# Next block's x loaded into idle output places, and a reordered opening, in a fused matmul–GELU–matmul kernel

## The chip, the cores and the metric

The kernel runs on one core of one Trainium2 chip. Its metric is the device time in microseconds (us), median of several runs: 881.87 us before the change, from three runs between 881.13 and 882.86. A lower time is better.

The engines are named as the profile names them: PE is the matrix engine (PEld its weight loads), DVE the vector engine, ACT the scalar engine, POOL the GpSimd engine, SP the sync engine, which here only issues transfers. "SPq", "ACTq" and "POOLq" are the transfers that those three engines issue; each has one queue of transfers, and an engine issues them in its own program order. All queues use the same 16 DMA engines.

## The reference

```python
x: (16, 512, 768)   w1: (768, 3072)   b1: (3072,)   w2: (3072, 768)      # float32
y = np.matmul(x, w1) + b1
y = 0.5 * y * (1.0 + erf(y / np.sqrt(2.0)))          # exact GELU
return np.matmul(y, w2).astype(np.float32)
```

So 8192 rows of x go through a product, a bias, a GELU and a second product.

## The kernel before

**Blocks of rows.** The 8192 rows are cut into ten blocks of 768 rows (six tiles of 128) and a last one of 512. A block's x lies in SBUF transposed, as `xt` (bf16; there is one such buffer). The GELU's output lies in `g`, and the output of the second product is collected in `ot`, which has four places of 128 x 768 float32 each.

**First product.** Blocks 1 to 10 use a two-by-two Strassen-like scheme: seven products P1 to P7 (line 154) for each of 12 pairs of column groups j, on sums of parts of w1 and sums of parts of x. The sums of x (`sum_x`, into `xft`) are made by DVE, the sums of w1 once (`make_w1`), stored to DRAM (`w1f`) and streamed back through a ring of five slots (`fill_slot`, on the SP queue, once for each j). Block 0 and a part of block 1 use plain products (line 396) instead, while the sums of w1 are being formed. ACT applies bias and GELU (line 143).

**Second product.** Three row tiles make a group: G0 and G1 in each block. A group's three-by-three-by-two product takes 15 products M0 to M14 of eight matmuls each (line 229), which add up in a few PSUM banks. Seven of them open a bank (M14, M8, M4, M7, M6, M13, M5). After a product, `finish2` copies the bank into a half of an output place (ACT, line 102) or adds it there (DVE, line 109); after M3, M11 and M0 a whole row tile is stored by POOL (line 237). A bank is used again by a later product of the same group: M12 goes on in M4's bank, M2 in M14's, M1 in M13's, so M12 must wait until M4 has been copied out, and so on.

**Places.** Group G0 of every block keeps its row 1 in place 0, row 2 in place 3, row 3 in place 2; G1 keeps row 1 in place 2, row 2 in place 1, row 3 in place 0. The first writes into them are the copies: M4 writes the first half of row 3, M13 its second half, M14 the first half of row 2, M6 its second half.

**The next block's x.** `prepare_x` loads each of the next block's six tiles with POOL into `xb` (a pool of two buffers, float32 turned into bf16 on the way) and transposes it with a DMA transpose on the SP queue from `xb` into `xt`. I call the six transposes T0 to T5. They may only start when the last product that reads `xt` has run. A third load waits until T0 has freed its buffer, and so on. `prepare_x` is called after M14 of group G0 in blocks 1 to 9, and ahead of group G0's products in block 0. In block 0 the order of the opening products is different: M4, M14, M13, M8, M7, M6 are fed together, and their copies follow in that order.

**The opening.** x tiles 0 and 1 come as float32 into places 2 and 3 (one on the SP queue, one on the ACT queue), are cast by DVE, and are transposed by PE (`turn_x0`). Until they arrive PE runs filler matmuls on zeros (`busy(n)`). Tiles 2 to 5 and the weights come on the POOL queue. Block 0's first products (`first`, line 459) use the first half of the first weight group, and then go on as the pieces arrive.

**Stores of the w1 sums.** The first four sums are kept in idle memory and stored at the end of block 0's first product by four transfers that ACT issues (`waiting`).

The order of the work is written out by hand: each engine executes its instructions in the order of the program, and waits are put in by the framework wherever regions of memory overlap.

Of the kernel before, what the change touches and what calls it, by code (L numbers as in the profile page):

```python
# [9 lines left out]
BF16 = mybir.dt.bfloat16  # L10
# [23 lines left out]
def kernel(  # L34
# [40 lines left out]
    def inorder(ins):  # L75
        return tc.keep_in_program_order(ins)

    def dma(queue, out, in_):
        inorder(queue.dma_start(out=out, in_=in_))  # L79
# [199 lines left out]
        ns = w // P  # L279
        return n // ns, (n % ns) * P  # L280

    def prepare_x(r0, w):
        for n in range(2 * w // P):
            xb = xbp.tile([P, K], BF16, name="xb")
            dma(nc.gpsimd, out=xb[:], in_=xf[r0 + n * P:r0 + (n + 1) * P, :])
            half, c0 = place(w, n)
            inorder(nc.sync.dma_start_transpose(out=xt[:, :, half, c0:c0 + P], in_=xb[:]))

    def sum_x(k, w):
        a11, a12 = xt[:, :KH, 0, :w], xt[:, KH:, 0, :w]  # L290
# [57 lines left out]
    def make_w1():  # L348
        nonlocal made
        n = made  # L350
        made += 1
        j = order1[n]
        a = raw(j)
        area, o = stage[n]
        s = area[:, o:o + SLOT].rearrange("p (f kc c) -> p f kc c", f=7, kc=KH)
        copy("act", s[:, 0:2], a[:, 1:3])

        def one():
            add(s[:, 2], a[:, 1], a[:, 2])
            add(s[:, 3:5], a[:, 0:4:2], a[:, 1:4:2])  # L360

        def two():
            sub(s[:, 5], a[:, 2], a[:, 0])
            sub(s[:, 6], a[:, 1], a[:, 3])
            if n < 4:
                waiting.append(lambda: dma(nc.scalar, out=w1f[j], in_=area[:, o:o + SLOT]))
            else:
                dma(nc.sync if n < 6 else nc.gpsimd, out=w1f[j], in_=area[:, o:o + SLOT])
            formed.add(j)
            if j in (9, 10):  # L370
                where[seq.index(j)] = area[:, o:o + SLOT]

        return one, two
# [52 lines left out]
    ident32 = words(stf, 2432, P)  # L426
    xw = ot[:, 2:4, :]
    dma(nc.sync, out=xw[:, 0, :], in_=xf[0:P, :])
    dma(nc.sync, out=b1s, in_=b1.rearrange("(hc p) -> hc p", p=P))
    dma(nc.scalar, out=xw[:, 1, :], in_=xf[P:2 * P, :])  # L430
    load_w1(0, 0, KH)
    inorder(nc.vector.memset(warm, 0.0))
    inorder(nc.scalar.activation(out=b1t[:, 0:1], in_=warm[:, 0:1], func=ACTF.Gelu))
    busy(7)
    make_identity(nc, ident32)
    copy("pool", ident, ident32)
    load_x0(2)
# [41 lines left out]
    MIDDLE = ("M12", "M2b", "M10a", "M11a", "M11b")  # L479

    copy("dve", xb0[:, 0, :], xw[:, 0, :])
    copy("dve", xb0[:, 1, :], xw[:, 1, :])
    turn_x0(0, "dve")
    tb = bank()
    inorder(nc.tensor.transpose(out=tb[:, :HC], in_=b1s, identity=ident32[:HC, :HC]))
    copy("act", b1t[:], tb[:, :HC])
    turn_x0(1, "dve")
    busy(4)
    first(0, 0, KH)
    first(1, 0, KH)  # L490
    turn_x0(2, "dve")
# [38 lines left out]
    make_w2(7)  # L530
    for m in ("M1", "M3b", "M10a", "M10b", "M11a", "M11b"):
        gsum(blk[0], m)
    for f in waiting:
        f()


    ts = [[dict() for _ in range(HP)] for _ in pairs]
# [22 lines left out]
    for p, (r0, w) in enumerate(pairs):  # L560
        nxt = pairs[p + 1] if p + 1 < len(pairs) else None
        G0, G1 = blk
        blk = groups(p + 1) if nxt is not None else None
        full = len(G1["tiles"]) == 3

        if p > 0:
            js = seq[:HP - PLAIN] if p == 1 else list(range(HP))
            last = len(js) - 1
            more = []
            if p == 1:  # L570
                hcs = [hc for j in range(PLAIN) for hc in (j, HP + j)]
                for n, hc in enumerate(hcs):
                    if n in (0, 1, 3):
                        form_w1()
                    if n in (1, 2):
                        sum_x(2 * n - 2, w)
                        sum_x(2 * n - 1, w)
                    plain(hc, 0)
                    if n == len(hcs) - 1:
                        ahead(p)  # L580
                    plain(hc, 1)
                free_slots(PLAIN)
                more = [0, 1, 3]

            both = (G0, G1) if full else (G0,)
            todo = [(js.index(QH - 1) if QH - 1 in js else 0, f) for G in both for f in gsums(G, *EARLY)]
            todo += [(js.index(2 * QH - 1), f) for G in both for f in gsums(G, *MIDDLE)]
            if p == 1:
                todo[2:4] = [(3, f) for _, f in todo[2:4]]

            halves = []

            def fill(s):
                if s in more and not halves:
                    more.remove(s)
                    halves.extend(make_w1())
                    halves.append(None)
                if halves and halves[0] is None:
                    halves.clear()
                elif halves:  # L600
                    halves.pop(0)()
                    if len(halves) == 1:
                        halves.clear()
                        free_slots(PLAIN)
                    return
                if s <= last and todo and s > todo[0][0] + (p > 1 or todo[0][0] > 0):
                    todo.pop(0)[1]()

            def step1(s, m):
                if 0 <= s <= last:  # L610
                    product1(ts[p][js[s]], m, p, js[s], w)

            for s in range(last + 1):
                if s == 0:
                    order = ((0, "P2"), (0, "P4"), (-1, "P1"), (0, "P6"))
                elif s == 1:
                    order = ((0, "P7"), (1, "P5"), (0, "P2"), (1, "P3"), (0, "P4"), (0, "P6"))
                else:
                    order = ((0, "P1"), (0, "P7"), (1, "P5"), (0, "P2"), (1, "P3"), (0, "P4"), (0, "P6"))
                for d, m in order:  # L620
                    step1(s - d, m)
                    if m in ("P2", "P6"):
                        fill(s)
            step1(last, "P5")
            part2(G0, "M14", range(0, 5))
            step1(last, "P3")
            part2(G0, "M14", range(5, QC))
            finish2(G0, "M14")
            if nxt is not None:
                prepare_x(*nxt)  # L630
            rest(G0, "M8")
            rest(G0, "M4")
            run([f for _, f in todo] + gsums(G0, *LATE))
            rest(G0, "M7")
            qs = [h * QH + q for q in range(QH) for h in range(2)]
            part2(G0, "M6", qs)
            finish2(G0, "M6")
            part2(G0, "M13", qs)
            finish2(G0, "M13")
        else:  # L640
            raws = ("M4", "M14", "M13", "M8", "M7", "M6")
            prepare_x(*nxt)
            for c in range(QC - 1):
                for m in raws:
                    part2(G0, m, (c,))
            for m in raws:
                part2(G0, m, (QC - 1,))
                finish2(G0, m)

        due = (gsums(G1, *EARLY, *MIDDLE) if p == 0 else []) + (gsums(G1, *LATE) if full else [])  # L650

        def take(n):
            r = due[:n]
            del due[:n]
            return r

        middle(G0, lambda n: take(1) if n >= 5 else [])
        rest(G0, "M0")

        if full:  # L660
            run(take(9))
            for m in ("M14", "M8", "M4"):
                rest(G1, m)
            if p > 0:
                for k in range(4):
                    sum_x(k, nxt[1])
            for m in ("M7", "M6", "M13"):
                rest(G1, m)
            if p == 0:
                form_w1()  # L670
            middle(G1, lambda n: [form_w1] if p == 0 and n == 5 else [])
            if p > 0:
                ahead(p + 1)
            rest(G1, "M0")
        else:
            a = lambda k: block(G1, 0, k)
            d12, d13 = st[:, 4, :, :], st[:, 5, :, :]
            sub(d12, a(0), a(1))
            sub(d13, a(0), a(2))
            t = ot[:, G1["o"][2], :]  # L680
            for n, terms in enumerate(((("b31", a(2)), ("M4", a(1)), ("b11", d12)),
                                       (("M13", a(2)), ("b22", a(1)), ("b12", d13)))):
                ps = bank()
                for f, lhs in terms:
                    for c in range(QC):
                        inorder(nc.tensor.matmul(  # L686
                            out=ps[:, :NB], lhsT=lhs[:, c, :], rhs=w2t[:, c, WF[f], :],
                            start=(f == terms[0][0] and c == 0), stop=(f == terms[2][0] and c == QC - 1)))
                copy("act", t[:, n * NB:(n + 1) * NB], ps[:, :NB])
                store(t, G1["rows"][0], True, n * NB, (n + 1) * NB)  # L690
# [30 lines left out]
```

## Time and profile before

| what | value |
|---|---|
| median of three runs | 881.87 us |
| the profiled execution's own time | 880.96 us |
| its span | 879.2 us |
| PE busy | 870.6 us (99%) |
| DVE / ACT / POOL busy | 587.6 / 397.9 / 84.6 us |
| PE's clock | 0.999 of full speed |
| DMA, mean | 168 GB/s |

The span is the time from the first to the last instruction in the profile; the device time stands 1.8 us above it in the profiled execution. The profiled execution itself is 0.91 us below the median of the runs. PE busy at 99% with the full clock says that the kernel can only be made shorter by taking away matmuls, or by taking away the remaining moments in which PE waits. A change that adds a wait to PE makes it longer by as much.

### The profile page before, as it was taken

Reading aid. Unit: us, or ns where it says so; the run is one execution under the profiler, and the core shown is the slowest. Engines: PE = TensorE matmul, PEld = TensorE weight load, DVE = VectorE, ACT = ScalarE, POOL = GpSimd, SP = SyncE. Lnnn points to the kernel's source line nnn. Section 1 sums busy time; section 2 is a strip of 40 time slices with the busy share of each in tenths; the row PEclk is TensorE's granted clock in tenths of the full one; section 3 lists DMA queues with packets and bytes.
Section 4 is the critical chain, followed back from the end, with each engine's and each line's share of the span. In section 5 each row is a group of like instructions: output and inputs, shape, how many; then the busy total and the mean of one; then the engine's idle time right before and its main releaser. Section 6 shows DMA issues by size and latency. Waiting matters only on the chain.

```text
span 879.2 us, 14061 instructions
## 1 busy us (share of the span) xinstructions
PE 870.6 (99%) x5505; PEld 532.6 (61%) x5505; DVE 587.6 (67%) x1105; ACT 397.9 (45%) x788; POOL 84.6 (10%) x153
## 2 busy tenths in 40 slices
PE   8999999999999999999999999999999999999998
PEld 6665556666666666666666666666666666666774
DVE  2888777757765766677577666756765766577654
ACT  3741384157227613741671276147316712751560
POOL 6201110110100011000001100110100011000000
PEclk9999999999999999999999999999999999999999
DMA  9998588566836664664668276556646683662621
GB/s 198 207 230 157 211 294 237 102 194 194 157 103 207 207 126 131 201 175 101 192 211 171 70 217 196 118 146 209 155 103 211 197 167 90 206 190 72 204 72 72
DMA packets 89031, 147.31 MB, mean 168 GB/s; under 512 B 50796, under 2 KB 68228, under 8 KB 88964
## 3 DMA queue, kind: packets, MB, share of 16 engines
q1 hardware_dynamic: 64148, 93.91, 37.2%
q0 software_dynamic: 24096, 49.36, 24.8%
q10 hardware_dynamic: 720, 3.15, 1.1%
q8 instruction: 43, 0.70, 0.3%
q14 instruction: 24, 0.20, 0.1%
HBM read 123.19 MB, written 33.42 MB: 178 GB/s over the span
## 4 chain that ended last, share of the span: by engine, by line
PE 93%; DMA 2%; DVE 2%; ACT 1%; issue 1%; POOL 0%; DVEq 0%; POOLq 0%; ACTq 0%
PE ps L229 44%; PE ps L154 42%; PE ps L396 5%; PE ps L686 1%; ACT g L143 1%; DMA w1f<-st 1%; PE ps L459 1%; DMA out_dram<-ot 1%; DMA ot<-in_x_dram 0%; DVE ot L109 0%; DMA xt<-xb 0%; ACT ot L102 0%; DVE st L112 0%; PE ps L421 0%; DVE ps L112 0%
## 5 line engine op out<-in xcount | busy, mean ns | idle before, releaser
L154 PEld LDWEIGHTS <-w1t 128*128 128x128 bf16 x2415 | 236.1, 98 | 145.6 <-issue 1.9
L143 ACT ACTIVATE g<-ps,b1t 128x384 bf16<-128x384 f32 (+1 forms) x411 | 222.8, 571 | 78.8 <-PE ps L154 56.4
L154 PE MATMUL ps<-xft,w1t 128*128 128x384 bf16 (+1 forms) x1380 | 257.4, 320 | 0.6 <-ACT ps L102 0.6
L229 PE MATMUL ps<-w2t,g 128*128 128x384 bf16 x1512 | 257.6, 326 | 0.3 <-DVE ot L109 0.3
L229 PEld LDWEIGHTS <-g 128*128 128x128 bf16 x1512 | 147.9, 98 | 98.0 <-issue 0.7
L154 PE MATMUL ps<-xt,w1t 128*128 128x384 bf16 (+1 forms) x1035 | 201.1, 320 | 0.2
L109 DVE TENSOR_TENSOR ot<-ot,ps 128x384 f32<-128x384 f32 x231 | 124.2, 552 | 81.1 <-PE ps L229 45.2
L229 PE MATMUL ps<-w2t,st 128*128 128x384 bf16 x1008 | 170.7, 326 | 0.7 <-ACT ot L102 0.7
L102 ACT COPY ot<-ps 128x384 f32<-128x384 f32 x128 | 60.4, 481 | 232.9 <-PE ps L229 203.7
L229 PEld LDWEIGHTS <-st 128*128 128x128 bf16 x1008 | 98.6, 98 | 66.1 <-issue 1.0
L102 ACT COPY ps<-ps 128x384 f32<-128x384 f32 (+1 forms) x117 | 53.0, 453 | 134.3 <-PE ps L154 134.3
L112 DVE TENSOR_TENSOR ev<-ps,ev 128x384 f32<-128x384 f32 (+1 forms) x117 | 63.7, 544 | 71.3 <-PE ps L154 70.4
L112 DVE TENSOR_TENSOR ps<-ps,ev 128x384 f32<-128x384 f32 (+1 forms) x117 | 64.7, 553 | 44.3 <-PE ps L154 43.8
L104 DVE COPY ev<-ps 128x384 f32<-128x384 f32 (+1 forms) x117 | 63.4, 542 | 23.0 <-PE ps L154 22.9
L79 POOL DMA_DIRECT2D xb<-in_x_dram x58 | 31.2, 541 | 472.8 <-DMA xt<-xb 465.1
L143 ACT ACTIVATE g<-ev,b1t 128x384 bf16<-128x384 f32 (+1 forms) x117 | 70.9, 606 | 11.4 <-DVE ev L112 11.4
L112 DVE TENSOR_TENSOR st<-g 128x1024 bf16<-128x1024 bf16 x107 | 73.1, 684 | 0.9 <-ACT g L143 0.9
L112 DVE TENSOR_TENSOR g<-g 128x1024 bf16<-128x1024 bf16 x84 | 57.5, 685 | 0.4
L79 POOL DMA_DIRECT2D out_dram<-ot x60 | 32.6, 544 | 225.0 <-DVE ot L109 224.9
L396 PE MATMUL ps<-xt,w1t 128*128 128x384 bf16 x252 | 41.6, 326 | 0.0
L396 PEld LDWEIGHTS <-w1t 128*128 128x128 bf16 x252 | 24.6, 98 | 16.2
L109 DVE TENSOR_TENSOR g<-g 128x1024 bf16<-128x1024 bf16 x42 | 29.0, 690 | 1.1
(67 smaller groups left out, 249.6 us busy)
## 6 DMA issues: line engine op xcount, KB each, us to landing
w1t<-w1f SPq DMA_DIRECT2D x115, 672.0 KB, 4.9
out_dram<-ot POOLq DMA_DIRECT2D x60, 384.0 KB, 3.7
xb<-in_x_dram POOLq DMA_DIRECT2D x58, 192.0 KB, 4.1
w2t<-in_w_dram POOLq DMA_DIRECT2D x8, 576.0 KB, 22.6
w1f<-st POOLq DMA_DIRECT2D x4, 672.0 KB, 6.8
w1t<-in_w_dram POOLq DMA_DIRECT2D x4, 576.0 KB, 22.4
w1f<-ot POOLq DMA_DIRECT2D x2, 672.0 KB, 5.1
w1t<-in_w_dram POOLq DMA_DIRECT2D x4, 288.0 KB, 6.2
```

What stands on the lines that cost most here:

```text
L79: inorder(queue.dma_start(out=out, in_=in_))
L102: inorder(nc.scalar.copy(out=dst, in_=src))
L104: inorder(nc.vector.tensor_copy(out=dst, in_=src))
L109: inorder(nc.vector.tensor_tensor(out=dst, in0=a, in1=b, op=ALU.add))
L112: inorder(nc.vector.tensor_tensor(out=dst, in0=a, in1=b, op=ALU.subtract))
L143: inorder(nc.scalar.activation(out=g[:, place_h(hc), half, :w], in_=src, func=ACTF.Gelu, bias=b1t[:, hc:hc + 1], scale=sign))
L154: inorder(nc.tensor.matmul(out=ps[:, :w], lhsT=forms[:, W1F[m], kc, :], rhs=moving1(m, kc, w), start=(kc == 0 and m in ("P1", "P7")), stop ...
L229: inorder(nc.tensor.matmul(out=ps[:, :NB], lhsT=lhs[:, c, :], rhs=w2t[:, c, WF[m], :], start=(m in OPENS and c == 0), stop=(c == QC - 1), ...
L396: inorder(nc.tensor.matmul(out=py[:, :HW], lhsT=lhs[:, kc, (j % 3) * P:(j % 3 + 1) * P], rhs=xt[:, kc, half, :], start=(kc == 0), stop=(kc ...
L459: inorder(nc.tensor.matmul(out=ps[:, c0:c0 + P], lhsT=w1_group(0)[:, kc, hc * P:(hc + 1) * P], rhs=xt[:, kc, half, c0:c0 + P], start=(c0 = ...
L686: inorder(nc.tensor.matmul(out=ps[:, :NB], lhsT=lhs[:, c, :], rhs=w2t[:, c, WF[f], :], start=(f == terms[0][0] and c == 0), stop=(f == ter ...
```

## The change

Four things are changed.

1. `prepare_x` takes a list of three places, one for each pair of x tiles. Where the entry is a number, the pair is loaded into that place of `ot` (each tile takes half a place, as bf16) and transposed from there; where it is `None`, the pair goes through `xb` as before. In block 0 the pairs go to place 2, place 3 and `xb`; in block 1 to `xb`, place 1, `xb`; in blocks 2 to 9 to place 2, `xb`, place 1.
2. Of the four stores of w1 sums at the end of block 0's first product, ACT issues two as before; SP issues the other two, behind T0 to T5.
3. x tiles 0 and 1 both come on the SP queue, the bias on the ACT queue. ACT casts tile 1 instead of DVE, behind nothing but its table load.
4. Fillers: ten instead of seven ahead of the first transpose, two new ones between the transposes of tile 0 and the bias, two instead of four ahead of the first products.

```diff
-    def prepare_x(r0, w):
+    def prepare_x(r0, w, places):
         for n in range(2 * w // P):
-            xb = xbp.tile([P, K], BF16, name="xb")
-            dma(nc.gpsimd, out=xb[:], in_=xf[r0 + n * P:r0 + (n + 1) * P, :])
+            at = places[n // 2]
+            o = None if at is None else (2 * at + n % 2) * K
+            xb = xbp.tile([P, K], BF16, name="xb")[:] if at is None else otf[:, o:o + K]
+            dma(nc.gpsimd, out=xb, in_=xf[r0 + n * P:r0 + (n + 1) * P, :])
             half, c0 = place(w, n)
-            inorder(nc.sync.dma_start_transpose(out=xt[:, :, half, c0:c0 + P], in_=xb[:]))
+            inorder(nc.sync.dma_start_transpose(out=xt[:, :, half, c0:c0 + P], in_=xb))
...
-                waiting.append(lambda: dma(nc.scalar, out=w1f[j], in_=area[:, o:o + SLOT]))
+                waiting.append(lambda queue: dma(queue, out=w1f[j], in_=area[:, o:o + SLOT]))
...
     dma(nc.sync, out=xw[:, 0, :], in_=xf[0:P, :])
-    dma(nc.sync, out=b1s, in_=b1.rearrange("(hc p) -> hc p", p=P))
-    dma(nc.scalar, out=xw[:, 1, :], in_=xf[P:2 * P, :])
+    dma(nc.sync, out=xw[:, 1, :], in_=xf[P:2 * P, :])
+    dma(nc.scalar, out=b1s, in_=b1.rearrange("(hc p) -> hc p", p=P))
...
-    busy(7)
+    busy(10)
...
     copy("dve", xb0[:, 0, :], xw[:, 0, :])
-    copy("dve", xb0[:, 1, :], xw[:, 1, :])
     turn_x0(0, "dve")
+    copy("act", xb0[:, 1, :], xw[:, 1, :])
+    busy(2)
...
     turn_x0(1, "dve")
-    busy(4)
+    busy(2)
     first(0, 0, KH)
...
-    for f in waiting:
-        f()
+    for f in waiting[:2]:
+        f(nc.scalar)
...
-                prepare_x(*nxt)
+                prepare_x(*nxt, (None, G1["o"][2], None) if p == 1 else (G0["o"][3], None, G1["o"][2]))
...
-            prepare_x(*nxt)
+            prepare_x(*nxt, (G0["o"][3], G0["o"][2], None))
+            for f in waiting[2:]:
+                f(nc.sync)
```

## The prediction

> **What bounds the kernel now.** I read the page's busy times first, then the list of who waited for whom with PE as the waiting engine, then the timeline where those waits lie, then the transfers' times to landing.
>
> ```profile
> PE 870.6 (99%) x5505; PEld 532.6 (61%) x5505; DVE 587.6 (67%) x1105; ACT 397.9 (45%) x788; POOL 84.6 (10%) x153
> ```
>
> PE is the bound; 8.6 us of the 879.2 us span are not PE's, the head and the last store among them. PE's own waits, in full but for the first (1.2, for the zeros that the fillers work on); the columns are the total in us, how often, and the longest:
>
> ```profile
> PE ps L421 <- DVE st L104: 1.3, 1, 1.3
> ...
> PE ps L229 <- ACT ot L102: 0.7, 1, 0.7
> PE ps L459 <- DVE xt L104: 0.6, 1, 0.6
> PE ps L154 <- ACT ps L102: 0.6, 2, 0.4
> PE ps L229 <- DVE ot L109: 0.3, 1, 0.3
> ```
>
> So all that can be won is about 3 us (0.3%), in the opening (1.3 and 0.6) and in blocks 0 and 1 (0.7, 0.6, 0.3). In blocks 2 to 9 PE waits for nothing. POOL's 465 us and DVE's 32 us of waiting for the transposes, the largest waits of the list, therefore cost nothing, and taking them away gives nothing by itself.
>
> The opening, in the timeline (start, duration, engine, line, operation, and in brackets the idle time before and what ended it):
>
> ```profile
> 5.05 1.04 DVE L104 CAST st<-ot 128x768 bf16<-128x768 f32 x2 [3.92 <-DMA ot<-in_x_dram]
> ...
> 5.67 0.51 PE L421 MATMUL ps<-st 128*128 128x128 bf16 x6 [1.31 <-DVE st L104]
> ...
> 6.28 0.51 PE L421 MATMUL ps<-st 128*128 128x128 bf16 x6
> 6.62 1.03 PE L406 MATMUL ps<-st 128*128 128x512 bf16 x4
> 7.49 1.17 PE L459 MATMUL ps<-xt,w1t 128*128 128x128 bf16 x18
> ```
>
> x tile 0 lands at 5.03, the cast takes 0.52, the transposes start at 5.67, and the first useful product at 7.49, behind the four fillers.
>
> Block 0's second product, lines of several engines:
>
> ```profile
> 56.87 27.82 SPq L287 DMA_TRANSPOSE xt<-xb  x6
> ...
> 63.80 2.39 ACT L102 COPY ot<-ps 128x384 f32<-128x384 f32 x6 [6.41 <-PE ps L229]
> ...
> 64.41 5.36 PE L229 MATMUL ps<-w2t,st 128*128 128x384 bf16 x32
> ...
> 65.22 0.53 POOL L79 DMA_DIRECT2D xb<-in_x_dram  x1 [25.80 <-DMA xt<-xb]
> ...
> 78.34 1.64 POOL L79 DMA_DIRECT2D out_dram<-ot  x3
> ...
> 83.28 0.48 ACT L102 COPY ot<-ps 128x384 f32<-128x384 f32 x1 [5.19 <-DMA out_dram<-ot]
> ...
> 84.81 5.36 PE L229 MATMUL ps<-w2t,st 128*128 128x384 bf16 x32 [0.74 <-ACT ot L102]
> ```
>
> POOL sits on x loads (the third waits for T0 until 65.22), so G0's three finished rows go out only at 78.34; G1's M8 copy needs place 2 and waits 5.19 us; PE then waits 0.74. Early loads take this chain away. But the same lines show the new one: M4's and M14's copies, the first two of the six that start at 63.80, write into places 2 and 3, from which the changed kernel transposes.
>
> A later block:
>
> ```profile
> 301.77 11.44 SPq L287 DMA_TRANSPOSE xt<-xb  x4
> ...
> 304.45 0.48 ACT L102 COPY ot<-ps 128x384 f32<-128x384 f32 x1 [0.82 <-PE ps L229]
> ...
> 307.27 1.19 POOL L79 DMA_DIRECT2D xb<-in_x_dram  x2 [42.79 <-DMA xt<-xb]
> ...
> 308.15 4.06 PE L229 MATMUL ps<-w2t,st 128*128 128x384 bf16 x24
> ```
>
> Here 304.45 is M4's copy, 307.27 shows T0 landed, 308.15 is M12, the first product that needs M4's bank back.
>
> Times from issue to landing of single transposes, from the transfers' view of short windows: T0 of block 0 (beside four stores), T2 of block 3 (nearly alone), T4 of block 1 (beside row stores):
>
> ```profile
> xt<-xb SPq DMA_TRANSPOSE x1, 7.8
> ...
> xt<-xb SPq DMA_TRANSPOSE x1, 2.7
> ...
> xt<-xb SPq DMA_TRANSPOSE x1, 6.1
> ```
>
> **The opening's cost.** Tiles 0 and 1 now move one behind the other on SP. Before 3.0 us the two queues had moved 0.11 and 0.04 MB, after it 436 GB/s together. If tile 0's remaining 0.28 MB goes alone, its data end near 3.65 instead of 4.45, and it lands near 4.3; if the order brings nothing, at 5.03. I take 4.4. Its cast ends at 4.95. The seven fillers follow each other every 0.43 us (the last starts at 3.73), the four later ones every 0.215, so ten end at 5.46, or nearer 5.0 if the last run fast: tile 0's transposes start about 0.3 earlier. The second tile decides: the same bytes have moved by then, so it lands at 5.2 as now (4.5 after its issue). ACT's cast has no row; bounds are DVE's 0.52 and 0.96, twice ACT's copy of 384 float32 (0.48). I take 0.83, ACT's copy of 128x768 bf16, as the same count of elements. PE turns tile 1 at 6.1 instead of 6.28 and has two fillers (0.43) fewer behind it, so the first product starts near 6.9. Its weights land at 1.27 + 5.3 = 6.6. Bounds: -0.75 to +0.2 (tile 1 half a microsecond late, slow cast). I take -0.5. The two new fillers lie in the time of ACT's cast, and the bias is early. The gain lasts: every later weight group lands about 3 us before its products start (group 2 at 18.6 for 21.5).
>
> [...]
>
> **Blocks 0 and 1, what goes.** POOL issues six loads without waiting, as soon as its earlier transfers allow (two of them at 36 and 39 now); the row stores then leave with DVE's adds, near 73 instead of 78.34, and land before M8's copy at 78.9. The 0.74 goes. DVE idled 3.85 us in that wait; with it done its backlog near 94 goes, and so the 0.28. Of the 0.6 in block 1 (ACT late by a row store that lets DVE and ACT go on only at 102.4) I take half, 0.3: that store stays, only DVE comes earlier. Together -1.3; bounds -1.6 and 0 (if the stores stay late).
>
> **Block 0, what comes.** M4's copy now waits for T0, M13's for T1, M14's for T2, M6's for T3, and on ACT the copies queue in the order M4, M14, M13, M8, M7, M6. M2 continues M14's bank. A product's eight matmuls take 1.30 us (0.1625 each, 227 in 36.89 in the chain), so M2 is due at 64.41 + 1.30 - 0.5 = 65.2, and with the copy's 0.48 T2 must land by 64.7. SP issues T0 at 56.87 still, since its tile lands just before. T0 and T1 cost SP 1.86 and 3.47 here, 1.2 each elsewhere; so T2 issues between 59.4 and 62.3, its data being there by then (the queue brings a tile each 0.9 us behind 57.7). Landing after 2.7 (alone) to 7.8 (four stores): 62.1 to 70.1, a wait of 0 to 5.4. There are two stores instead of four, but also four loads; the row nearest to this traffic is 6.1, and ACT's fewer issues speak for an early one, 60.0: T2 lands at 66.1, PE waits 1.4. M12's own wait for T0 (by 63.4; 56.87 + 6.1 = 63.0) lies ahead of it and is not added. The two stores moved behind T5 on SP have only SP's stores from 87.5 on behind them; their memory is written again at 85.8, some 10 us after they land.
>
> **Later blocks.** T0 lands 5.5 us after its issue at most (307.27 less 301.77); M4's copy, pushed from 304.45 to there, ends at 307.75 ahead of M12 at 308.15. Nothing queues on ACT behind it but copies that have time. Bounds: zero, and, were T0 to take 6.7 as T4 of block 0 did, 0.8 in each of eight blocks. I take 0: the same two slot fills lie ahead of T0 as now. The four earlier loads fall beside the slot fills, which land 6.3 us after issue where loads lie beside them now and are needed some 11 us after it.
>
> **Sum**, against the profiled execution: 880.96 - 0.5 - 1.3 + 1.4 = 880.6. That execution lies 0.91 under the median of the runs, so 881.4 against 881.87.
>
> **Rivals.** A, faster: the transposes land by 64.7, as a T2 issued at 59.4 beside little traffic would; no wait appears, 881.87 - 1.8 = 880.1, to 879.2 if the opening gives 0.75 and block 1 all its 0.6. For it: two stores fewer. Against it: even T0, first in line, took 7.8.
>
> B, slower: in block 0 three queues (POOL's loads, ACT's stores, SP's transposes) share the DMA engines where the stores and the transposes took them before, and T2, third in its queue, lands like T0 did with 7.8 or later. From a landing at 68.3 it decides: 3.6 of wait less 1.8 is +1.8. At 62.3 + 7.8 = 70.1 it is 881.87 + 5.4 - 1.8 = 885.5; a middle of it is 884. [...]
>
> C, slower: M4's copy in blocks 2 to 9 comes too late by 0.3 to 0.8 each, since T2 to T5 now crowd behind T0: 883.5 to 888.
>
> **How the numbers follow.** 0.2% (1.76 us) is about what a measurement of this kernel can tell from no change. My forecast (gain and new wait nearly cancel, 880.2 to 883.6) has 0.44, A 0.33, B 0.16, C 0.07. So faster 0.33, same 0.44, slower 0.23. The range 879.2 to 884.6 reaches over A and the nearer half of B and C.
>
> **What will show it.** Right: L459 starts near 6.9; the wait of 0.74 near 84 is gone; M14's copy in block 0 shows a wait for a transpose, and PE one for ACT of about 1.4 near 65; PE waits nowhere in blocks 2 to 9; POOL's wait for transposes shrinks with no effect. Wrong: no PE wait near 65 (A), one over 3.6 (B), or waits of PE for ACT once per block (C).

## The result, and the profile after

The changed kernel takes 886.69 us (median of seven executions, 883.21 to 889.63) against 881.75 us for the kernel before, timed beside it (seven, 881.09 to 882.86). The ratio is 1.0057, with a 95% interval of 1.0031 to 1.0083: slower by more than the 0.2% that can be told from no change. The forecast of 881.4 us and the upper end of the range, 884.6, both lie below it. The profiled execution took 889.43 us and is one of the longest; the same kernel also ran in 883.2 us, so it now spreads over 6.4 us. The rows below are those of this one execution; no shorter one was profiled. The experiments find a cause for a part of the spread.

The page's head and busy times:

```profile
span 887.7 us, 14117 instructions
...
PE 874.1 (98%) x5508; PEld 533.6 (60%) x5508; DVE 588.7 (66%) x1104; ACT 397.6 (45%) x789; POOL 84.5 (10%) x153
```

The span is 8.5 us longer and PE is busy 3.5 us longer, for three more matmuls. So PE waits more, and some of its matmuls also take longer. PE's waits (total in us, how often, the longest):

```profile
PE ps L229 <- ACT ot L102: 6.5, 3, 5.8
PE ps L408 <- DVE st L434: 1.2, 1, 1.2
PE ps L461 <- DMA w1t<-in_w_dram: 0.8, 1, 0.8
PE ps L461 <- DVE xt L104: 0.6, 1, 0.6
PE ps L154 <- ACT ps L102: 0.5, 1, 0.5
```

The wait of 1.3 for tile 0's cast in the opening is gone, and so are those of 0.7 and 0.3 in block 0 and near 94. One of 5.8 for ACT's copies has come, and the first products (line 461, 459 before) now wait for their weights. Block 0's second product in the timeline (start, duration, engine, line, operation; in brackets the idle time before and what ended it):

```profile
56.80 13.11 SPq L289 DMA_TRANSPOSE xt<-ot  x4
56.94 7.96 PE L229 MATMUL ps<-w2t,g 128*128 128x384 bf16 x48
...
57.15 0.36 ACTq L79 DMA_DIRECT2D w1f<-ot  x1
...
57.60 0.57 ACTq L79 DMA_DIRECT2D w1f<-st  x1
...
70.13 0.48 ACT L102 COPY ot<-ps 128x384 f32<-128x384 f32 x1 [12.41 <-DMA xt<-ot]
70.66 7.95 PE L229 MATMUL ps<-w2t,st 128*128 128x384 bf16 x32 [5.75 <-ACT ot L102]
...
70.94 0.15 PEld L229 LDWEIGHTS <-st 128*128 128x128 bf16 x1 [0.17 <-issue]
71.26 0.15 PEld L229 LDWEIGHTS <-st 128*128 128x128 bf16 x1 [0.17 <-issue]
...
71.42 2.01 ACT L102 COPY ot<-ps 128x384 f32<-128x384 f32 x5 [0.81 <-DMA xt<-ot]
```

The six opening products end at 64.9, 0.3 later than before. ACT's first copy, M4's, begins at 70.13, because place 2 is still being read by T0. M12, which needs M4's bank, starts at 70.66 after 5.75 us of idle PE. The second thing to see is the 7.95 us of the 32 matmuls that follow: before, the same 32 took 5.36 us. The weight loads, one ahead of each matmul, come 0.32 us apart (70.94, 71.26, and so on), where matmuls of this form follow each other every 0.163 us at full speed. Sixteen come at that half rate, up to 76.0, and cost 2.6 us.

T0's own landing, from the transfers' view of 56.75 to 56.9 (count, and us from issue to landing):

```profile
xt<-ot SPq DMA_TRANSPOSE x1, 13.2
```

It lands at 70.03; T1, T2 and T3 follow at 70.67, 71.32 and 72.00. ACT's two stores, issued just behind T0, land at 68.46 and 69.95. All that was put on the DMA engines at 56.8 to 57.6 finishes within two microseconds of 70.

The opening (PE):

```profile
3.72 1.30 PE L408 MATMUL ps<-st 128*128 128x512 bf16 x4
4.86 0.50 PE L423 MATMUL ps<-st 128*128 128x128 bf16 x6
...
5.89 0.51 PE L423 MATMUL ps<-st 128*128 128x128 bf16 x6
...
7.60 1.18 PE L461 MATMUL ps<-xt,w1t 128*128 128x128 bf16 x18 [0.77 <-DMA w1t<-in_w_dram]
```

x tiles 0 and 1 land at 3.98 and 4.95 and the transposes start 0.8 and 0.4 earlier than before, but the first weights land at 7.55 (6.58 before), so the first product starts at 7.60 instead of 7.49.

Blocks 5 and 6 have a small wait each. Block 5's:

```profile
469.12 2.65 SPq L289 DMA_TRANSPOSE xt<-ot  x2
...
475.56 1.63 ACT L102 COPY ot<-ps 128x384 f32<-128x384 f32 x4 [4.58 <-DMA xt<-ot]
476.09 3.09 PE L229 MATMUL ps<-w2t,st 128*128 128x384 bf16 x18 [0.43 <-ACT ot L102]
```

T0 took 6.3 us to land there, against 4.8 in block 3, where nothing waits.

The account of the span: block 0's second product starts 0.3 later than before (56.94 for 56.61), its wait costs 5.75 and the half rate 2.6, blocks 5 and 6 cost 0.7 (6.5 in three waits, 5.8 of it in one), and 0.74 and 0.28 are gone: 8.3 of the 8.5 us.

### The profile page after: what moved, and what is told of

Same layout as the page of the kernel before. It is cut to its first block, busy times and chain, and to the rows that moved or that the text cites. A ratio compares the mean times of both kernels' runs of the same rounds, so it can differ in the third digit from the quotient of the medians.

```text
span 887.7 us, 14117 instructions
## 1 busy us (share of the span) xinstructions
PE 874.1 (98%) x5508; PEld 533.6 (60%) x5508; DVE 588.7 (66%) x1104; ACT 397.6 (45%) x789; POOL 84.5 (10%) x153
## 4 chain that ended last, share of the span: by engine, by line
PE 91%; DMA 4%; ACT 2%; DVE 1%; issue 1%; DVEq 0%; ACTq 0%; POOLq 0%
PE ps L229 44%; PE ps L154 41%; PE ps L398 5%; DMA xt<-ot 3%; PE ps L691 1%; ACT g L143 1%; DMA w1f<-st 1%; PE ps L461 1%; DMA w1t<-in_w_dram 1%; DVE st L112 1%; ACT ot L102 0%; DVE ev L112 0%; DVE ps L112 0%; ACT st L102 0%; PE ps L423 0%
## 5 line engine op out<-in xcount | busy, mean ns | idle before, releaser
L229 PE MATMUL ps<-w2t,st 128*128 128x384 bf16 x1008 | 173.3, 329 | 6.5 <-ACT ot L102 6.5
L79 POOL DMA_DIRECT2D out_dram<-ot x60 | 32.7, 546 | 663.8 <-DVE ot L109 660.8
L109 DVE TENSOR_TENSOR st<-st,g 128x1024 bf16<-128x1024 bf16 x42 | 28.9, 688 | 0.8
```

The source lines that it names most:

```text
L109: inorder(nc.vector.tensor_tensor(out=dst, in0=a, in1=b, op=ALU.add))
L229: inorder(nc.tensor.matmul(out=ps[:, :NB], lhsT=lhs[:, c, :], rhs=w2t[:, c, WF[m], :], start=(m in OPENS and c == 0), stop=(c == QC - 1), ...
```

## The experiments

Edits are shown against the changed kernel unless the text says otherwise. Each ratio is to the kernel before, timed on the same chip beside it: 881.18 us for the two halves, block 0 through `xb` and the four stores behind, 880.94 for the fillers and for the three with one store on ACT, and 881.01 for the last two. The ratio is taken over the executions and need not be the quotient of the two medians.

### The two halves of the change

First the change without its opening: before's order of the first loads, before's fillers and before's cast, with all the rest of the change.

```diff
-    dma(nc.sync, out=xw[:, 1, :], in_=xf[P:2 * P, :])
-    dma(nc.scalar, out=b1s, in_=b1.rearrange("(hc p) -> hc p", p=P))
+    dma(nc.sync, out=b1s, in_=b1.rearrange("(hc p) -> hc p", p=P))
+    dma(nc.scalar, out=xw[:, 1, :], in_=xf[P:2 * P, :])
...
-    busy(10)
+    busy(7)
...
-    copy("act", xb0[:, 1, :], xw[:, 1, :])
-    busy(2)
...
```

> The change of prepare_x and of the stores, with the opening of before. Theory 1 (in block 0 M4's copy into place 2 waits for T0, which lands 13 us after its issue beside two stores; PE stands 5.8 us and then runs 32 products at half clock, 2.6 us more): as the changed kernel, 883 to 890, with PE waiting for ACT near 64 for 3 to 6 us. Rival 1 (the opening loses the time, its first weights land 1 us later): near 882. Rival 2 (M4's copy is late in blocks 2 to 9): also 883 to 890, but with PE waits of 0.3 to 0.8 in several of those blocks that sum to most of it.

Measured: 885.91 us (884.08 to 888.29), ratio 1.0051 (1.0034 to 1.0068). Its profiled execution is its quickest, and PE shows it twice in block 0:

```profile
66.53 1.46 PE L229 MATMUL ps<-w2t,st 128*128 128x384 bf16 x8
69.40 2.76 PE L229 MATMUL ps<-w2t,st 128*128 128x384 bf16 x16 [1.41 <-ACT ot L102]
72.67 1.47 PE L229 MATMUL ps<-w2t,st 128*128 128x384 bf16 x8 [0.51 <-DVE st L109]
```

Here T0 landed after 4.3 us and M12 did not wait, but T1, T2 and T3 landed at 68.3 to 69.4 and M2 waited 1.4. The second wait, of 0.51 for a sum that DVE makes for M5, is one more consequence: DVE's additions need ACT's copies, stand late in its queue, and M5's sum stands behind them. No product runs at half rate here.

Then the opening alone, with before's x loads and stores.

```diff
-    def prepare_x(r0, w, places):
+    def prepare_x(r0, w):
...
-    for f in waiting[:2]:
-        f(nc.scalar)
+    for f in waiting:
+        f()
...
```

> The opening of the changed kernel, all else as before. Theory 1: within 0.5 us of before (first product at 7.6 at the latest), 881.3 to 882.3. Rival 1: 885 or more. If the late first weights (7.55 instead of 6.58) were chance, the first product starts near 6.9 and the time is 881.2.

Measured: 880.81 us (879.69 to 885.81), ratio 1.0000 (0.9986 to 1.0014). The opening neither gains nor loses. Its profile shows why it gains nothing:

```profile
7.09 0.59 PE L406 MATMUL ps<-st 128*128 128x512 bf16 x2
8.49 1.18 PE L459 MATMUL ps<-xt,w1t 128*128 128x128 bf16 x18 [0.80 <-DMA w1t<-in_w_dram]
```

PE is done with the fillers before 7.7 and then waits for the weights, which land at 8.44. The whole loss is in the x and store part.

### Which transfers hold up block 0's transposes

Block 0's x through `xb` again, the later blocks and the stores as changed. This takes the early loads away from the stores and transposes. It also frees the copies from the transposes, so the time would recover however late T0 were; what speaks for the loads is T0's own landing.

```diff
-            prepare_x(*nxt, (G0["o"][3], G0["o"][2], None))
+            prepare_x(*nxt, (None, None, None))
```

> The changed kernel with block 0's call given no places, so that block 1's x goes through xb as before; two stores stay behind the transposes. Theory 1: no wait of PE near 65, the old wait of 0.7 near 84 may return; 880.5 to 882.5, and the spread between executions falls from 6 to about 1 us. Rival 2: 884 or more stays.

Measured: 881.25 us (880.33 to 884.54), ratio 1.0004 (0.9993 to 1.0015). The loss is gone, though one execution still took 884.54. T0, beside two stores but no early loads, lands after

```profile
xt<-xb SPq DMA_TRANSPOSE x1, 5.5
```

Next, all four stores on SP behind T5, so that the transposes meet the loads alone.

```diff
-    for f in waiting[:2]:
-        f(nc.scalar)
...
-            for f in waiting[2:]:
+            for f in waiting:
                 f(nc.sync)
```

> The changed kernel with all four stores of w1 sums issued by SP behind T0 to T5. If the two stores on ACT's queue hold up the transposes, T0 lands within 6 us of its issue and T2 by 65, PE waits under 1 us near 64, and the time is 879.5 to 881.5, less than before. If the four loads hold them up, T0 lands 10 us or more after its issue as in the changed kernel, PE waits 3 us or more, and the time is 883 or more. M8's copy then waits for the first store, which could cost up to 1 us.

Measured: 888.87 us (887.83 to 889.65), ratio 1.0084 (1.0070 to 1.0098), the slowest of all. But the transposes were quick, T0 landing 5.6 us after its issue and T1 to T3 at 63.5 to 65.0. A new wait took the old one's place:

```profile
64.47 1.24 ACT L102 COPY ot<-ps 128x384 f32<-128x384 f32 x3 [6.41 <-PE ps L229]
65.08 4.06 PE L229 MATMUL ps<-w2t,st 128*128 128x384 bf16 x24
66.25 0.53 SPq L79 DMA_DIRECT2D w1f<-ot  x1
...
70.90 1.24 ACT L102 COPY ot<-ps 128x384 f32<-128x384 f32 x3 [5.20 <-DMA w1f<-ot]
71.80 1.48 DVE L109 TENSOR_TENSOR ot<-ot,ps 128x384 f32<-128x384 f32 x3 [6.89 <-ACT ot L102]
...
73.94 2.74 PE L229 MATMUL ps<-w2t,st 128*128 128x384 bf16 x8 [4.80 <-DVE st L109]
```

M12, M2 and M1 run on time. The first store now lands at 70.8, and it reads place 0 and a part of place 1, into which M8 and M7 are copied. Their copies wait, M6's waits behind them on ACT, DVE's additions wait for them, and M5's sum, behind the additions on DVE, comes 4.8 us late. My expectation had allowed at most 1 us for this, because it followed the copies to PE but not through DVE's queue. As a test of the transposes the run still counts: without stores beside them they land in time.

One store on ACT, three on SP behind the transposes:

```diff
-    for f in waiting[:2]:
+    for f in waiting[:1]:
...
-            for f in waiting[2:]:
+            for f in waiting[1:]:
```

> The changed kernel with only the first store (which M7's and M8's copies wait for) on ACT, the other three on SP behind T0 to T5. If stores and transposes beside each other are what makes T0 late, and the first store's landing behind the transposes is what cost 4.8 us when all four were moved, both waits shrink: T0 lands by 65, T2 by 67, PE waits 0 to 2.5 us near 64, 880 to 883.

Measured: 884.71 us (882.12 to 886.63), ratio 1.0037 (1.0020 to 1.0053). In its profile T0 took

```profile
xt<-ot SPq DMA_TRANSPOSE x1, 10.4
```

and landed at 67.58, within 0.02 us of the one store (67.60). The expectation, T0 by 65 and 880 to 883, was missed. So T0 from issue to landing took 13.2 us beside two stores and the loads, 10.4 beside one store and the loads, 5.6 beside the loads alone, 5.5 beside two stores alone. In these traces the loads alone or two stores alone leave T0 in time. Both together do not, except in the x part alone, where T0 was issued 1 us ahead of the first store and took 4.3; T1, issued there with the second store, took 8.9. How far ahead of the stores T0 is issued was not tested on its own. Four stores without loads are no longer harmless: in the first profile of before T0 took 7.8 beside them, and T1, which had an x load beside it too from 65.22 on, took 11.5.

Leaving the four stores out would have been the cleanest run. It was not tried, since the sums' memory would then be read unwritten.

### The half rate after a long wait

Eighteen idle matmuls between the opening products and M12, in a bank that is not yet in use, so that PE is not idle while it waits:

```diff
+            G0["5"] = bank()
+            for _ in range(18):
+                inorder(nc.tensor.matmul(out=G0["5"][:, :NB], lhsT=w2t[:, 0, 0, :P], rhs=w2t[:, 0, 0, :],
+                                         start=True, stop=True))
```

> The changed kernel with 18 filler products (2.9 us) on PE in block 0 between its first six products and M12, where PE would wait. [...] If the wait alone makes up the slow executions, they stay at 889.

Measured: 885.30 us (885.24 to 885.48), ratio 1.0050 (1.0035 to 1.0066). The spread over executions falls from 6.4 us to 0.24. PE's lines:

```profile
65.18 3.09 PE L656 MATMUL ps<-w2t 128*128 128x384 bf16 x18
...
68.11 1.46 PE L229 MATMUL ps<-w2t,st 128*128 128x384 bf16 x8
...
70.70 2.76 PE L229 MATMUL ps<-w2t,st 128*128 128x384 bf16 x16 [1.12 <-ACT ot L102]
...
73.97 1.48 PE L229 MATMUL ps<-w2t,st 128*128 128x384 bf16 x8 [0.51 <-DVE st L109]
```

M12 starts 2.93 us later than the opening products allow (68.11 for 65.18), and 1.12 and 0.51 follow: 4.6 us, against 4.4 measured. Nothing runs at half rate, although T0 took 9.5 us here. The granted clock of its executions is 0.999 or 1.0. In the changed kernel the executions with a clock of 1.0 took 883.2 and 883.4 us, those with 0.998 took 886.2 and 886.7, and those with 0.995 and 0.996 took 889.1 to 889.6. So the longest executions are those with the lowest granted clock, and in the profiled one, 889.43, which is among them, PE ran at half clock after its wait. There the half rate makes 2.6 of the 6.4 us. The rest is probably the wait itself, which the fillers even out too, since they hide any landing of T0 ahead of about 67.5; the short executions have no profile that would show it.

Long idle times of PE can be set against the clock behind them: 5.75 us was followed by 16 slow matmuls, 4.80 us (four stores behind) by 9, 2.88 us (one store on ACT) by 9, and 1.41 us (x part alone) by none. The 2.88 in PE's line of the run with one store on ACT, 32 matmuls in 6.75 instead of 5.36:

```profile
68.21 6.75 PE L229 MATMUL ps<-w2t,st 128*128 128x384 bf16 x32 [2.88 <-ACT ot L102]
```

PE's granted clock in windows of 1 us shows where the half rate begins and ends (window, its length, the busy times of PE, PEld, DVE, ACT and POOL, then the clock, the DMA share and GB/s). In the changed kernel, and then with one store on ACT:

```profile
69.00:70.00 1.00, 0.00 (x0) 0.00 (x0) 0.00 (x0) 0.00 (x0) 0.00 (x0) 0.56 1.10 114
...
75.00:76.00 1.00, 1.00 (x4) 0.44 (x3) 0.18 (x2) 0.00 (x0) 0.00 (x0) 0.52 1.04 430
```

```profile
67.00:68.00 1.00, 0.00 (x0) 0.00 (x0) 0.00 (x0) 0.32 (x1) 0.00 (x0) 0.82 1.13 238
...
71.00:72.00 1.00, 1.00 (x7) 0.60 (x6) 1.00 (x4) 0.00 (x0) 0.00 (x0) 0.97 0.96 357
```

The windows between these have 0.50, those outside 1.00. Worked out from the four rows, the clock was halved from 69.1 to 76.0, 6.8 us, and from 67.6 to 71.1, 3.4 us. The first fall came 4.2 us after PE's last matmul (64.9), the second 2.3 us after it (65.3). So an idle time of 2.88 us was enough; what sets the moment of the fall and the length of the half rate, no run shows.

### Can the early loads be had without the loss?

The first store by ACT some 5 us earlier, ahead of the last plain products, and the other three behind the transposes:

```diff
+    waiting[0](nc.scalar)
...
-    for f in waiting[:2]:
-        f(nc.scalar)
...
-            for f in waiting[2:]:
+            for f in waiting[1:]:
```

> As before, but the first store is issued by ACT one weight group earlier, near 50 us, when its data have been ready for 20 us; the other three on SP behind T0 to T5. No store stands beside the transposes: T0 lands 5.6 us after its issue or sooner, no wait of PE over 0.5 us near 65, 879.5 to 881.0. Cost: the last second-product weights and block 1's x land up to 1.7 us later, which DVE has some 3 us of room for.

Measured: 882.44 us (881.80 to 883.80), ratio 1.0021 (1.0012 to 1.0030). The expectation, at most 881.0, was missed. T0 takes 5.5 us with no store issued beside it, and every execution has a clock of 0.999 or 1.0. But the store now moves beside the loads of block 1's x, T0 is issued at 60.56 instead of 56.80, and waits stay in block 0 (0.8 and 0.5) and one later block (0.4):

```profile
PE ps L229 <- ACT ot L102: 1.2, 2, 0.8
...
PE ps L229 <- DVE st L109: 0.5, 1, 0.5
```

Then the same, with only place 1 used in blocks 2 to 9, so that M4's copy is never behind a transpose there:

```diff
-                prepare_x(*nxt, (None, G1["o"][2], None) if p == 1 else (G0["o"][3], None, G1["o"][2]))
+                prepare_x(*nxt, (None, G1["o"][2], None))
```

> The last kernel, and blocks 2 to 9 use block 1's pattern (xb, place 1, xb), so that M4's copy waits for no transpose. The two waits of PE of 0.5 to 0.6 in blocks 5 and 6 go: 1 us less than the kernel with the early store alone, 878.5 to 880.5. If those waits were chance and belong to no cause of the places, nothing changes between the two.

Measured: 881.76 us (880.99 to 882.23), ratio 1.0008 (0.9998 to 1.0017); 880.5 at most was expected. In its profile PE no longer waits for ACT's copies, and the median is 0.7 us lower. The edit accounts for the 0.4 of the later block alone: block 0's 0.8 is gone in this profile too, though the edit does not touch it, and the two intervals overlap. Last, that kernel with before's opening (against the one just told of):

```diff
-    dma(nc.sync, out=xw[:, 1, :], in_=xf[P:2 * P, :])
+    dma(nc.scalar, out=xw[:, 1, :], in_=xf[P:2 * P, :])
...
-    busy(10)
+    busy(7)
...
-    copy("act", xb0[:, 1, :], xw[:, 1, :])
+    copy("dve", xb0[:, 1, :], xw[:, 1, :])
...
```

> The kernel with one early store, M4's places avoided in blocks 2 to 9, and now with before's opening: only the x change is left, with its wait for M14, M13 and M5's sum in block 0. With the new opening this was 1.0008 (0.9998 to 1.0017). If the opening is worth nothing, as when it was run alone (1.000), this is 880.5 to 882.5, ratio 0.9995 to 1.0015. If the late weights belong to the new opening and cost it 0.5 to 1.3, this is 880.0 to 881.0 and the ratio lies 0.0006 to 0.0015 lower than with the new opening, at or under 1. If avoiding the waits of 0.74, 0.28 and part of 0.6 in blocks 0 and 1 is worth 1.3 net of the 0.5 for M5's sum, 0.999. It shows whether any form of the x change beats the kernel before by more than the bound.

Measured: 881.03 us (880.44 to 882.28), ratio 1.0001 (0.9992 to 1.0010). So the early loads can be had without the loss, but no gain can be told from nothing. No version that I ran beats the kernel before.

### How much of a single profile can be believed

The kernel before, unchanged, profiled a second time.

> The kernel before, unchanged, profiled once more, to see how much of the opening belongs to the execution and not to the change. In the profile of before the first weights landed at 6.58 us; in the five kernels with the new opening whose profiles I looked at for it, between 7.55 and 9.0, but in the kernel with before's opening and the new x loads also at 7.47. If the landing of the first weights differs from execution to execution whatever the opening, this profile has it anywhere between 6.6 and 9.0, likely over 7.0, and the first product starts behind it. If the reordered queues are what delays the weights, it lands at 6.6 again and the first product starts at 7.5. The ratio is 1.000 either way, within 0.001; waits of PE for ACT of 0.7 near 84 and of 0.3 near 94 return in both cases.

Measured: 881.46 us (879.37 to 883.43), ratio 1.0002 (0.9992 to 1.0012); the profiled execution took 881.38 us, its span 879.6. PE's waits, in full but for one of 1.2 for the fillers' zeros:

```profile
PE ps L421 <- DVE st L104: 1.2, 1, 1.2
...
PE ps L459 <- DVE xt L104: 0.6, 1, 0.6
PE ps L154 <- ACT ps L102: 0.4, 1, 0.4
```

The waits of 0.7 near 84 and 0.3 near 94, of which the prediction made most of its gain, are not there. My expectation that they would return was wrong. T0 was issued 1 us ahead of ACT's first store this time and landed in 2.9 us instead of 7.8. And the opening differs:

```profile
5.61 0.82 PE L421 MATMUL ps<-st 128*128 128x128 bf16 x6 [1.25 <-DVE st L104]
...
7.20 1.91 PE L406 MATMUL ps<-st 128*128 128x512 bf16 x4
8.90 1.38 PE L459 MATMUL ps<-xt,w1t 128*128 128x128 bf16 x11
```

The four fillers took 1.91 us instead of 1.03, and the first product starts at 8.90 instead of 7.49, though the weights were there at 6.76. PE ran at half rate there: 11 products took 1.38 us, where 18 took 1.17 in the first profile. Of the four profiles with seven fillers two show this (the x part alone is the other). In the eight with ten, the two fillers ahead of the first product took 0.59 us each time, PE's full rate. So the first profile of before had a quick opening and 1.0 us of waits, the second a slow opening and neither wait, and the spans are 879.2 and 879.6.

The first weights landed at 6.58 and 6.76 in the two profiles of before, at 7.47 and 7.46 in the two kernels with before's opening and the new x loads (x part alone, and the last kernel with the early store), and at 7.55 to 9.0 in the eight with the new opening. Whether the new order of the queues holds the weights up, or part of it is chance, stays open: it is a difference between single profiles, and the opening alone measured 1.0000.

## Why the prediction was wrong

**What bounds the kernel: right, but read from one execution.** PE is the bound, and taking away POOL's 465 us of waits gave nothing: POOL's largest wait is now 660.8 us for DVE's rows, at no cost. The list of PE's waits, though, was that of one execution. The term of -1.3 for blocks 0 and 1 was credited from it. The 0.74 and 0.28 did go in the changed kernel, but the second profile of before lacks them too; of block 1's 0.6, a wait of 0.5 stayed, where half was to go. The last kernel with the early store, which has neither 0.74 nor 0.28 and pays 0.5 for M5's sum, measured 1.0001 (0.9992 to 1.0010), where -1.3 + 0.5 would be 0.9991. Its profile also has a new wait of 0.9 for weights near 17, so this comparison does not decide the matter alone.

**The opening, -0.5: wrong.** Its first steps came out: tile 1 landed at 4.95 (5.2 said), ACT's cast took 0.83 as taken, and the ten fillers ended at 5.02, where 5.46, or nearer 5.0, was said. In the other seven profiles of this opening they ended between 5.15 and 5.64, so that is partly luck. The step that failed is "Its weights land at 1.27 + 5.3 = 6.6", a landing taken over unchanged while other transfers were reordered. They landed at 7.55 and the first product came at 7.60 instead of 6.9. By the run with the opening alone it is worth 0.0.

**Block 0's new wait, +1.4: the step that decided the result.** The mechanism was right, copies in ACT's order behind transposes that read their places. The failing step is the landing: "the row nearest to this traffic is 6.1", which gave T0 63.0 and T2 66.1. T0 took 13.2 us and landed at 70.03, and PE waited 5.75 us in the profiled execution instead of 1.4. The runs show that the loads or two stores alone leave T0 at 5.5 to 5.6 and both together bring it to 9.5 to 13.2, except where it was issued a full microsecond ahead of the first store (4.3). And the bound from 7.8 was too low by a row that was there. It was T0's; the six transposes that block 0 issues before the change have

```profile
DMA to landing us min/median/max: 2.8/5.6/11.5
```

and the 11.5 is T1's, which was issued 2 us behind T0 beside the same four stores and had all three queues at work beside it from 65.22 on, when POOL issued the third load. With it the wait would have been bounded by 62.3 + 11.5 - 64.7 = 9.1 us and not by 5.4. Nor was M2 the one to wait, as had been said: T0 landed hardly sooner than T2, and M12, the first product to need a copy, took the whole wait.

**A term that was missing: +2.6 in the profiled execution.** The prediction had two rates for the first fillers (one each 0.43 us, then each 0.215) and did not ask what a long wait would do to the matmuls behind it. Sixteen of them ran at half clock, 0.32 us each instead of 0.163. With fillers in the wait none did in the profile, and every execution took 885.2 to 885.5.

**Later blocks, 0 in eight: nearly right.** Two of the eight had a wait, 0.7 together, where T0 took 6.3 (5.5 at most was said, and 0.8 for 6.7). Rival C as worked out for all eight did not come.

**The rivals.** Rival B, at 0.16, came nearest: with three queues at work in block 0 the transposes were late, and T2 landed at 71.3 where B's later end was 70.1. Its path was another, though. B let M2 wait for T2; T0 itself was late, and M12 waited for it. Whether the three queues' sharing of the DMA engines is the reason, as B had it, no run shows. B's 885.5 leaves out the half clock, and that it lies only 1.2 under the 886.69 measured is in part luck. In rival A's sum, 881.87 - 0.75 - 1.6 gives 879.5, not 879.2, which changes nothing here.

## What to carry to other kernels

Before a copy is put behind a transfer, list every queue that will be moving at that moment; landing times of the same transfer beside other traffic are no bound for it, and here two neighbours that were harmless alone (5.5 and 5.6 us) brought it to between 9.5 and 13.2 us together, in three profiles of four. Take the bound from the largest row at that place, too, and not from the first transfer alone. A long wait of PE can cost a second time, in the matmuls behind it: here those of 2.88 us and more did, and one of 1.41 did not. And read PE's small waits in two profiles of the same kernel before counting them as a gain: here 1.0 us of them came and went with the execution.

## What the hardware did that I had not expected

- Transposes and stores that were in flight together often finished together: beside T0's landing at 70.03 a store landed at 69.95; 67.58 and 67.60 with one store on ACT; 64.66 and 64.47 in the first profile of before; in the second, T1 at 67.36 and a store at 67.15. In the run with fillers they were 0.4 apart, in block 0 through `xb` 1.0. The store that landed at 69.95 took 12.3 us from issue to landing, and 7.2 before the change, without early loads. But the last of the early loads was in at 63.06, 7 us ahead of T0, so the loads' own traffic is not all of it. Why they finish together no run shows.
- A transpose issued 1 us ahead of the first store landed in 2.9 and 4.3 us (the second profile of before, the x part alone); issued 0.35 us ahead with loads beside it, in 13.2 and 10.4. Single profiles again.
- PE at half clock: 0.32 us instead of 0.163 for each matmul, for 16, 9 and 9 of them after waits of 5.75, 4.80 and 2.88 us. The clock fell within the wait, 4.2 and 2.3 us into the first and the last of these.
